# Convolution taps released one projection earlier, five to three weight units, the norm one part later

## The chip, the cores and the metric

The kernel runs on one core of a Trainium2 chip. The metric is device time in microseconds (us) of one execution, 2061.1 us as the median of three runs of the kernel before (2060.99 to 2061.4). The core has five engines that work side by side and wait for each other through semaphores: TensorE (PE) multiplies, and its weight loads (PEld) overlap its multiplications; VectorE (DVE) and ScalarE (ACT) compute element by element; GpSimd (POOL) and SyncE (SP) issue transfers here. Each engine takes its instructions in an order that is fixed before the run.

## What is computed

A trunk of two layers on 256 tokens of 2048 features. In a layer three token mixers (A sparse attention, B a convolution module, C stick-breaking attention) read the same normalised input; each is gated and projected, the three are merged by sigmoid gates, projected once more and added to the input. The branch that matters here is B:

```python
def conformer_conv(u, conv_w, conv_b, ln_w, ln_b):
    a, gt = jnp.split(u, 2, axis=-1)
    y = a * jax.nn.sigmoid(gt)
    y = lax.conv_general_dilated(y, conv_w, window_strides=(1,), padding=[(CONV_WIDTH - 1, 0)],
                                 feature_group_count=CONV_CH) + conv_b      # depthwise, width 31
    y = layer_norm(y, ln_w, ln_b)
    return jax.nn.silu(y)

def hybrid_layer(x, ...):
    proj = rms_norm(x, norm_w) @ w_in
    (qa, ka, va, za, qi, ki, wi, ub, zb, qc, kc, vc, zc, gates) = jnp.split(proj, split_points(), axis=-1)
...
    y_a = (dsa_attention(qa, ka, va, qi, ki, wi, top_k) * jax.nn.silu(za)) @ w_a_out
    y_b = (conformer_conv(ub, ...) * jax.nn.silu(zb)) @ w_b_out
    y_c = (stick_breaking_attention(qc, kc, vc) * jax.nn.silu(zc)) @ w_c_out
    g = jax.nn.sigmoid(gates).reshape(b, s, N_BRANCH, D_MODEL)
    merged = g[:, :, 0] * y_a + g[:, :, 1] * y_b + g[:, :, 2] * y_c
    return x + merged @ w_out
```

The convolution has 1024 channels, which are 8 blocks of 128 partitions, and 31 taps: 248 products of a block with a tap's column of weights, in each layer. A final norm closes the trunk.

## The kernel before

**Weight units.** All weights are streamed once, in units of mostly 512 KB. `load_unit` (L193) issues a unit's transfer on SyncE's queue into one of four `raw` buffers. `high` (L216) rounds it on ACT into `wh`, and `low` (L220) subtracts on DVE what is left into `wl` (L222); three buffers of each. The products (L232, through `mult`) of a unit use `wh` twice, for the high and the low part of the activations, and `wl` once. `chunk_T` (L235), `chunk_N` (L332) and `chunk_first` (L302) run a projection over its units; a projection of 512 columns over the 2048 features has eight units of twelve matmuls. `unit` and its parts carry high priority.

**Work beside the units.** The order of each engine is made before the run by the framework's scheduler: what is ready is placed, high priority first, otherwise what was written earlier first. `tc.issue_after(ins)` ties the instructions of its block, as far as they are on `ins`'s engine, behind `ins`. Three lists bring work in between the units:
- `pending` (L142): what follows a `turned` projection. Its result is transposed in blocks on DVE, written to memory and read back on POOL's queue, and then used some ten units later.
- `stages` (L134): generators that `background` (L156) moves on by one part after a unit, each part asking for so many units before the next; their matmuls are tied behind the unit's last matmul. `finish` runs all that are left.
- `waiting` (L132): the convolution's taps. `taps` (L663) makes, for four of the eight channel blocks, the 124 calls in the order pair of blocks, tap, block of the pair, and cuts them into entries of two and one. `tap` (L420) is one DVE instruction of 128 x 256 elements: L424 for a block's first tap, L426 for the thirty that follow and add to the same accumulator `cv`. `drain` (L174) is called by `low` and issues one entry for each unit, tied behind that unit's subtraction, unless `hold` is set. `flush` (L185) issues all entries that are left, untied.

**The order of a layer.** First the two halves of the convolution's input (UG and UA, 512 columns each); `use_u` (L674) copies each half into `yT` (L675) and calls `taps`. Then `hold` is set (L700), and the indexer's queries QI (32 units of 256 columns, matmuls of 384 and 192 columns), its keys, the values VA and the keys KA of branch A follow. `index_first` and `index` (L735, L763) are stages that score the keys and pick the top 64 by eight rounds of a maximum and a replacement on DVE (`choose`, L727). Beside them run QA (the sparse branch's queries) and QC (the stick branch's), 16 units each. Then `hold` is cleared (L799), and KC, the gate ZA and VC follow (16 units each), with `attend` (L801) and `stick` (L865) as stages. Last the merge (L953): for each branch, in the order A, C, B, four parts `j` of 512 columns; a part has eight units of the gate and four of the branch's output projection. The gate ZC (16 units) stands ahead of branch A's last part, and ZB ahead of branch C's last part (`b == 2 and j == 3`). `flush` and the start of `conv_norm` (L913) stand ahead of branch C's second part (`b == 2 and j == 1`, L963).

**`conv_norm`.** A stage of three parts: sums over the channel blocks (L918, L919); three units later a matmul that makes the mean (L922), the subtraction (L925), squares and their sums (L928, L929); six units later the matmul for the variance (L932) and the rest. Its result in `cv` is what ZB's gate is multiplied with.

Of the kernel before, what the change touches and what calls it, by code (L numbers as in the profile page):

```python
# [48 lines left out]
def trunk(ctx: ExitStack, tc: tile.TileContext, x, w_in, xt, w_a, w_b, w_c, w_out,  # L49
# [38 lines left out]
    def nm(s):  # L88
        uid[0] += 1
        return f"{s}_{uid[0]}"  # L90

    def slot(dt=F32):
        return sp.tile([P, KC, S], dt, tag="s8", bufs=12, name=nm("s8"))
# [7 lines left out]
    def parts(n, own=()):  # L101
        own = list(own)
        return own + [slot(F32R).rearrange("p (k w) t -> p k w t", w=2) for _ in range(n // 4 - len(own))]
# [22 lines left out]
    def ev():  # L126
        return tp.tile([P, 512], F32, tag="ev", bufs=3, name=nm("ev"))

    def small(w=16, bufs=8):
        return tp.tile([P, w], F32, tag=f"sm{w}", bufs=bufs, name=nm("sm"))  # L130

    waiting = []  # L132
# [19 lines left out]
    def settle():  # L152
        while pending:
            step_on(pending[0])
# [10 lines left out]
    def start(gen):  # L165
        stages.append([gen, 0])

    def finish():
        while stages:
            advance(stages[0])  # L170

    hold = [False]
# [10 lines left out]
            it[0] -= 1  # L183

    def flush():  # L185
        while waiting:
            for f in waiting.pop(0)[1]:
                f()

    newest = [None]  # L190
    newest_parts = [None, None]
# [62 lines left out]
    def turned(srcs, use, later=LATER, tmp=None):  # L254

        n = len(srcs)
        if tmp is None:
            tmp = tp.tile([P, n * 512], F32, tag="zt", bufs=1, name=nm("zt"))  # L260
        tmp = tmp.rearrange("p (t b k i) -> p t b k i", b=4, k=4, i=32)
        z = dp.tile([n, 4, 32, 4, P], F32, tag="z", bufs=4, name=nm("z"))
        with tc.high_priority():
            for t, src in enumerate(srcs):
                nc.vector.transpose(tmp[:, t].rearrange("p b k i -> p k b i"),  # L265
                                    src.rearrange("p (k b c) -> p k b c", b=4, c=32))
            for a in range(4):
                nc.gpsimd.dma_start(z[:, :, :, a, :].rearrange("t b c e -> c (t b) e"),  # L268
                                    tmp[a * 32:(a + 1) * 32].rearrange("c t b k i -> c (t b) (k i)"))

        def rest():
            y = tp.tile([P, n * 4, 4, 32], F32, tag="zy", bufs=1, name=nm("zy"))
            nc.gpsimd.dma_start(y.rearrange("p (t a) k i -> p t (a k i)", t=n),  # L273
                                z.rearrange("t b c a e -> (b c) t (a e)"))
            yield later - 2
            yield from use(y)

        pending.append([count[0] + 2, rest()])
# [7 lines left out]
    def chunk_F(w, c0, act, nk, use, later=LATER):  # L286
        turned(chunk_N(w, [(c0, 512)], act, nk), use, later)
# [44 lines left out]
    def chunk_N(w, segs, act, nk, ku=2, accs=None, ks=None):  # L332
        n = sum(c for _, c in segs)
        if accs is None:
            accs = token_accs()
        for k0 in range(*(ks or (0, nk)), ku):
            background(token_products(accs, n, unit(w, k0, ku, segs), act, k0, ku, nk, range(NT)))
        return accs
# [70 lines left out]
    def gate(c0, o, b, w, hx):  # L409
        def use(k, y):  # L410
            sg = sigmoid_of(y)
            yield 1
            nc.vector.tensor_mul(y, y, sg)
            nc.vector.tensor_mul(y, y, blocks(o[:, k:k + 4, :]).rearrange("p k u i -> p u k i"))
            split(blocks(hi(b, k, 4)), blocks(lo(b, k, 4)), by_feature(y))

        for k in range(0, KC, 4):
            chunk_F(w, c0 + k * P, hx, KD, partial(use, k), LATER + 1 if k else LATER - 1)
# [55 lines left out]
    for layer in range(DEPTH):  # L474
# [188 lines left out]
        def taps(j, yT=yT, cv=cv, pr=pr):  # L663
            ops = []
            for c in range(j * 4, j * 4 + 4, 2):
                for q in range(TAPS):
                    for d in range(2):
                        ops.append(partial(tap, yT, cv, pr, c + d, q))
            while ops:
                n = 1 + (len(waiting) % 2 == 0)  # L670
                waiting.append([4, ops[:n]])
                ops = ops[n:]

        def use_u(j, y, yT=yT):  # L674
            nc.scalar.copy(blocks(yT[:, j * 4:j * 4 + 4, PAD:]), by_feature(y))  # L675
            taps(j)
            yield 0
# [109 lines left out]
        qaT = slot()  # L787
        for h in range(0, NH, 4):
            chunk_F(w, O_QA + h * P, hx, KD, partial(rope_F, qaT[:, h:h + 4, :]), LATER - 1)
        qcT = slot()  # L790

        def use_q(h, y, qcT=qcT):
# [3 lines left out]
        for h in range(0, NH, 4):  # L796
            chunk_F(w, O_QC + h * P, hx, KD, partial(use_q, h))
        finish()
        hold[0] = False  # L799

        def attend(t, c, qaT=qaT, kaT=kaT, va=va, bias=bias):  # L801
            n = (t + 1) * P
# [110 lines left out]
        def conv_norm(cv=cv, pr=pr):  # L913
            work = t4()
            red = [work[:, i * S:(i + 1) * S] for i in range(4)]
            sums = red[2:]
            for i in range(2):
                nc.vector.tensor_reduce(red[i], cv[:, i * 4:i * 4 + 4, :].rearrange("p c t -> p t c"), op=ALU.add, axis=AX.X)  # L918
            nc.vector.tensor_add(red[0], red[0], red[1])  # L919
            yield 3  # L920
            ps = mm_tile()
            nc.tensor.matmul(ps[:, :S], mean_w, red[0], start=True, stop=True)  # L922
            for i in range(2):
                cs = cv[:, i * 4:i * 4 + 4, :]
                nc.vector.tensor_sub(cs, cs, heads(ps[:, :S], 4))  # L925
                sq = t4()
                nc.scalar.activation(sq.rearrange("p (c t) -> p c t", c=4), cs, AF.Square)
                nc.vector.tensor_reduce(sums[i], sq.rearrange("p (c t) -> p t c", c=4), op=ALU.add, axis=AX.X)  # L928
            nc.vector.tensor_add(sums[0], sums[0], sums[1])  # L929
            yield 6  # L930
            vs = mm_tile()
            nc.tensor.matmul(vs[:, :S], mean_w, sums[0], start=True, stop=True)  # L932
            r = rsqrt_mean(vs[:, :S], 1, t4())
            for i in range(2):
                cs = cv[:, i * 4:i * 4 + 4, :]
                nc.vector.tensor_mul(cs, cs, heads(r, 4))
                sg = t4()
                for c in range(4):
                    cc = i * 4 + c
                    lw, lb = pr[:, P_LW + cc:P_LW + cc + 1], pr[:, P_LB + cc:P_LB + cc + 1]  # L940
                    nc.scalar.activation(sg[:, c * S:(c + 1) * S], cs[:, c, :], AF.Sigmoid, bias=lb, scale=lw)
                    nc.vector.tensor_scalar(cs[:, c, :], cs[:, c, :], lw, lb, op0=ALU.mult, op1=ALU.add)
                nc.vector.tensor_mul(cs, cs, sg.rearrange("p (c t) -> p c t", c=4))
# [9 lines left out]
        for b in (0, 2, 1):  # L953
            if b == 1:
                mx = parts(KD)
            gx = ga if b == 0 else gc if b == 2 else gb
            for j in range(4):

                if b == 0 and j == 3:
                    finish()  # L960
                    gc = parts(KC)
                    gate(O_ZC, qcT, gc, w, hx)
                if b == 2 and j == 1:  # L963
                    flush()
                    start(conv_norm())
                if b == 2 and j == 3:
                    finish()
                    gb = parts(KC)
                    gate(O_ZB, cv, gb, w, hx)
                g = chunk_N(w, [(O_G + b * D + j * 512, 512)], hx, KD)  # L970
                sg = [ev() for _ in range(NT)]
                with tc.high_priority():
                    for t in range(NT):
                        nc.scalar.activation(sg[t], g[t], AF.Sigmoid)  # L974
                if j == 0:
                    settle()
                y = chunk_N((w_a, w_b, w_c)[b][layer], [(j * 512, 512)], gx, KC)
                with tc.high_priority():
                    for t in range(NT):
                        dst = mg[j // 2][:, j % 2, t, :]  # L980
                        if b == 0:
                            nc.vector.tensor_mul(dst, y[t], sg[t])
                        else:
                            nc.vector.tensor_mul(sg[t], y[t], sg[t])  # L984
                            nc.vector.tensor_add(dst, dst, sg[t])  # L985
                if b == 1:
                    turned([mg[j // 2][:, j % 2, t, :] for t in range(NT)], partial(use_m, j), LATER - 2)
# [58 lines left out]
        c0, n = 1536, 256  # L1046
# [8 lines left out]
        c0, n = D - S, S  # L1055
# [5 lines left out]
        for t in range(NT):  # L1061
# [4 lines left out]
            m, r, b = (small(1) for _ in range(3))  # L1066
# [66 lines left out]
```

## Time and profile before

| | us |
|---|---|
| median of three runs | 2061.1 |
| the profiled execution | 2062.56 |
| its span, from the first to the last instruction | 2060.8 |
| PE busy in it | 2035.9 |
| DVE busy in it | 1504.4 |
| taps (L426, 480 in two layers) | 218.8, 478 ns each |
| subtractions (L222, the 729 of the main group) | 876.6, 1207 ns each |

The page lists busy times, the chain of waits that ended last, and the groups of instructions. A line of the timeline is start, duration, engine, line, operation, tiles written from tiles read, shape and count; in brackets stands how long the engine was idle before it, and what ended the wait. Several like instructions in a row are merged into one line with a count (`x6`). A stretch of the view by windows is its length and then, for each engine, busy time and count. Matmuls are pipelined, so that the duration of one is longer than the distance from its start to the next one's.

### The profile page before, as it was taken

What the parts mean: (1) busy time and instruction counts of PE and PEld (TensorE: products, weight loads), DVE (VectorE), ACT (ScalarE), POOL (GpSimd) and SP (SyncE); (2) the same over time, 40 slices, a digit from 0 to 9 for tenths busy, and PEclk for the clock granted to TensorE, in tenths of its full rate; (3) what the DMA queues carried; (4) which work ended last, traced back from release to release, by engine and by line L of the source; (5) the groups of instructions that cost most, each with busy time, mean ns of one, the idle gap of its engine ahead of it and who ended that gap; (6) DMA issues with size and microseconds to landing.
All of it is one profiled execution on the core that took longest, in us unless ns stands there. A gap on an engine that the chain in (4) does not pass through costs nothing.

```text
span 2060.8 us, 26151 instructions
## 1 busy us (share of the span) xinstructions
PE 2035.9 (99%) x9680; PEld 1721.7 (84%) x9680; DVE 1504.4 (73%) x2020; ACT 1042.1 (51%) x1223; POOL 119.2 (6%) x199
## 2 busy tenths in 40 slices
PE   9999999999999999999999899999999999999998
PEld 8889888888888788888888898888888887888887
DVE  8687878787778956555775879777886799566555
ACT  7455545466444544444554554554664445444443
POOL 0100011100010000010100000111000100000100
PEclk9999999999999999999999999999999999999999
DMA  7767586765576577776967675867655765676764
GB/s 264 226 201 225 179 245 194 234 191 168 175 234 194 174 217 236 213 234 215 307 200 232 184 212 184 247 185 233 195 164 181 233 189 182 214 250 212 245 223 152
DMA packets 246528, 435.03 MB, mean 211 GB/s; under 512 B 19712, under 2 KB 69888, under 8 KB 246272
## 3 DMA queue, kind: packets, MB, share of 16 engines
q1 hardware_dynamic: 231632, 389.32, 60.5%
q0 software_dynamic: 13104, 40.91, 6.5%
q10 hardware_dynamic: 1664, 3.15, 0.4%
q8 instruction: 75, 1.23, 0.2%
q14 instruction: 53, 0.43, 0.1%
HBM read 408.67 MB, written 24.64 MB: 210 GB/s over the span
## 4 chain that ended last, share of the span: by engine, by line
PE 94%; DVE 4%; issue 1%; ACT 0%; DVEq 0%; ACTq 0%
PE acc L232 90%; DVE wl L222 2%; DVE s L426 2%; PE mm L772 1%; PE mm L806 1%; PE mm L831 0%; PE mm L904 0%; PE mm L868 0%; PE mm L823 0%; PE mm L604 0%; DVE t L928 0%; PE mm L890 0%; PE mm L743 0%; PE mm L871 0%; PE mm L906 0%
## 5 line engine op out<-in xcount | busy, mean ns | idle before, releaser
L232 PE MATMUL acc<-wh,s 128*128 128x512 f32 (+2 forms) x5248 | 1283.6, 387 | 0.0
L222 DVE TENSOR_TENSOR wl<-raw,wh 128x1024 fp32r<-128x1024 f32 (+2 forms) x729 | 876.6, 1207 | 426.9 <-ACT wh L218 420.5
L218 ACT CAST wh<-raw 128x1024 fp32r<-128x1024 f32 (+2 forms) x728 | 758.2, 1043 | 845.1 <-PE acc L232 653.9
L232 PEld LDWEIGHTS acc<-wh,s 128*128 128x128 f32 x5248 | 971.0, 188 | 195.1 <-ACT wh L218 0.4
L232 PE MATMUL acc<-wl,s 128*128 128x512 f32 (+2 forms) x2624 | 692.2, 386 | 0.0
L232 PEld LDWEIGHTS acc<-wl,s 128*128 128x128 f32 x2624 | 487.8, 188 | 99.2
L426 DVE SCALAR_TENSOR_TENSOR s<-yT,cst,s 128x256 f32<-128x256 f32 x480 | 218.8, 478 | 3.0
L268 POOL DMA_DIRECT2D z<-zt x152 | 88.7, 590 | 1603.3 <-DVE zt L265 1453.4
L232 PE MATMUL acc<-s,wh 128*128 128x384 f32 (+1 forms) x608 | 129.4, 355 | 0.0
L232 PEld LDWEIGHTS acc<-s,wh 128*128 128x128 f32 x608 | 107.7, 194 | 3.2
L232 PEld LDWEIGHTS acc<-s,wl 128*128 128x128 f32 x608 | 80.2, 195 | 15.3 <-DVE wl L222 14.3
L232 PE MATMUL acc<-s,wl 128*128 128x192 f32 (+1 forms) x608 | 82.4, 279 | 10.4 <-DVE wl L222 10.3
L265 DVE STREAM_TRANSPOSE zt<-acc 128x512 f32<-128x512 f32 x48 | 34.1, 711 | 17.4 <-PE acc L232 17.4
L273 POOL DMA_DIRECT2D zy<-z x39 | 28.0, 719 | 253.3 <-DMA z<-zt 100.4
L367 DVE TENSOR_TENSOR s<-zy,s 128x1024 fp32r<-128x1024 f32 x20 | 24.4, 1220 | 21.6 <-ACT s L366 21.6
L366 ACT CAST s<-zy 128x1024 fp32r<-128x1024 f32 x20 | 21.0, 1051 | 29.1 <-DMA zy<-z 23.0
L984 DVE TENSOR_TENSOR ev<-acc,ev 128x512 f32<-128x512 f32 x32 | 21.9, 685 | 13.2 <-PE acc L232 13.2
L974 ACT ACTIVATE ev<-acc 128x512 f32<-128x512 f32 x48 | 26.5, 592 | 0.1
L391 DVE TENSOR_TENSOR ev<-ev,cst 128x384 f32<-128x384 f32 (+2 forms) x20 | 11.1, 557 | 17.4 <-ACT ev L389 17.2
L388 ACT COPY ev<-ev 64x384 f32<-64x384 f32 (+2 forms) x20 | 10.2, 511 | 25.9 <-DVE ev L293 25.7
L985 DVE TENSOR_TENSOR s<-s,ev 128x512 f32<-128x512 f32 x32 | 21.8, 683 | 0.0
L1016 DVE TENSOR_TENSOR t<-acc,t 128x512 f32<-128x512 f32 (+1 forms) x18 | 10.6, 627 | 13.8 <-PE acc L232 13.8
(206 smaller groups left out, 828.8 us busy)
## 6 DMA issues: line engine op xcount, KB each, us to landing
raw<-in_w_in_dram SPq DMA_DIRECT2D x555, 512.0 KB, 3.9
raw<-in_w_out_dram SPq DMA_DIRECT2D x64, 512.0 KB, 4.7
zy<-z POOLq DMA_DIRECT2D x39, 512.0 KB, 5.3
z<-zt POOLq DMA_DIRECT2D x152, 128.0 KB, 4.1
raw<-in_w_a_dram SPq DMA_DIRECT2D x32, 512.0 KB, 3.6
raw<-in_w_c_dram SPq DMA_DIRECT2D x32, 512.0 KB, 4.0
raw<-in_w_b_dram SPq DMA_DIRECT2D x32, 512.0 KB, 4.9
raw<-in_w_in_dram SPq DMA_DIRECT2D x16, 256.0 KB, 3.1
```

Source lines behind the costliest of these rows:

```text
L218: newest_parts[0] = nc.scalar.copy(u[1], u[0])
L222: newest_parts[1] = sub = nc.vector.tensor_sub(u[2], u[0], u[1].bitcast(F32))
L232: newest[0] = nc.tensor.matmul(o, lhsT, rhs, start=start, stop=stop, skip_group_check=True)
L265: nc.vector.transpose(tmp[:, t].rearrange("p b k i -> p k b i"), src.rearrange("p (k b c) -> p k b c", b=4, c=32))
L268: nc.gpsimd.dma_start(z[:, :, :, a, :].rearrange("t b c e -> c (t b) e"), tmp[a * 32:(a + 1) * 32].rearrange("c t b k i -> c (t b) (k i)"))
L273: nc.gpsimd.dma_start(y.rearrange("p (t a) k i -> p t (a k i)", t=n), z.rearrange("t b c a e -> (b c) t (a e)"))
L366: nc.scalar.copy(h, src)
L367: nc.vector.tensor_sub(l, src, h.bitcast(F32))
L426: nc.vector.scalar_tensor_tensor(o, yT[:, c, q:q + S], wq, o, op0=ALU.mult, op1=ALU.add)
L974: nc.scalar.activation(sg[t], g[t], AF.Sigmoid)
L984: nc.vector.tensor_mul(sg[t], y[t], sg[t])
L985: nc.vector.tensor_add(dst, dst, sg[t])
```

## The change

Four places, all about the taps. `hold` is cleared after QA instead of after QC, so that entries are issued from QC's first unit on. An entry holds one tap where the length of the list divides by three, and two otherwise, which is five taps in three units instead of three in two. `flush` and the start of `conv_norm` move from branch C's second part to its third. And what `flush` issues is tied behind the newest subtraction.

```diff
     def flush():
-        while waiting:
-            for f in waiting.pop(0)[1]:
-                f()
+        with tc.issue_after(newest_parts[1].ins):
+            while waiting:
+                for f in waiting.pop(0)[1]:
+                    f()
...
             while ops:
-                n = 1 + (len(waiting) % 2 == 0)
+                n = 1 + (len(waiting) % 3 > 0)
                 waiting.append([4, ops[:n]])
                 ops = ops[n:]
...
             chunk_F(w, O_QA + h * P, hx, KD, partial(rope_F, qaT[:, h:h + 4, :]), LATER - 1)
+        hold[0] = False
         qcT = slot()
...
         for h in range(0, NH, 4):
             chunk_F(w, O_QC + h * P, hx, KD, partial(use_q, h))
         finish()
-        hold[0] = False
...
-                if b == 2 and j == 1:
+                if b == 2 and j == 2:
                     flush()
                     start(conv_norm())
```

## The prediction

> **What bounds the kernel now.** I read the page's busy times and the chain of waits first.
>
> ```profile
> span 2060.8 us, 26151 instructions
> PE 2035.9 (99%) x9680; PEld 1721.7 (84%) x9680; DVE 1504.4 (73%) x2020; ACT 1042.1 (51%) x1223; POOL 119.2 (6%) x199
> PE acc L232 90%; DVE wl L222 2%; DVE s L426 2%; PE mm L772 1%; PE mm L806 1%; PE mm L831 0%; PE mm L904 0%; PE mm L868 0%; PE mm L823 0%; PE mm L604 0%; DVE t L928 0%; PE mm L890 0%; PE mm L743 0%; PE mm L871 0%; PE mm L906 0%
> ```
>
> TensorE (PE) is the bound: 2035.9 of 2060.8 us busy, 24.9 us idle. A change of VectorE's (DVE) order can only act where PE waits for DVE. The chain says there are such places, and that the low-part subtractions (L222) and the convolution taps (L426) stand in them with 2% each. So the next view is the busy time by stretch: length, then PE, weight loads, DVE, ACT, POOL, granted clock, DMA share, GB/s.
>
> ```profile
> 112.00:146.00 34.00, 29.87 (x183) 28.08 (x182) 31.48 (x57) 16.69 (x23) 0.00 (x0) 0.90 0.54 163
> 146.00:252.00 106.00, 105.98 (x640) 96.68 (x639) 84.33 (x152) 57.66 (x79) 3.04 (x5) 1.00 0.68 205
> 252.00:296.00 44.00, 44.00 (x196) 36.44 (x195) 32.63 (x39) 21.08 (x20) 6.09 (x10) 1.00 0.81 250
> 296.00:420.00 124.00, 124.00 (x567) 102.73 (x566) 94.96 (x133) 62.74 (x88) 14.52 (x24) 1.00 0.69 210
> 420.00:560.00 140.00, 140.00 (x642) 116.68 (x641) 111.34 (x160) 85.51 (x92) 0.72 (x1) 1.00 0.57 177
> 656.00:688.00 32.00, 32.00 (x142) 26.48 (x142) 30.55 (x47) 13.22 (x14) 0.00 (x0) 1.00 0.61 193
> 688.00:704.00 16.00, 13.45 (x58) 10.53 (x57) 15.46 (x18) 8.87 (x9) 0.00 (x0) 1.00 0.48 143
> 1134.00:1170.00 36.00, 29.74 (x181) 27.95 (x181) 32.80 (x59) 17.02 (x25) 0.00 (x0) 0.91 0.54 163
> 1712.00:1728.00 16.00, 13.45 (x58) 10.54 (x58) 15.21 (x17) 8.84 (x9) 0.00 (x0) 1.00 0.47 142
> ```
>
> PE is short in two places of each layer, and full between them: among the indexer's queries (112 to 146, and 1134 to 1170 in layer 1: 4.13 and 6.26 us idle, DVE nearly full, clock 0.90), and at the convolution's norm (688 to 704 and 1712 to 1728: 2.55 us idle each). These four hold 15.5 of the 24.9 us.
>
> **Which taps stand there.** The same view for L426 alone (DVE busy and count), then lines of DVE's timeline:
>
> ```profile
> 112.00:146.00 34.00, 14.49 (x30) 0.90 0.54 163
> 656.00:688.00 32.00, 14.48 (x30) 1.00 0.61 193
> 113.86 0.41 DVE L424 TENSOR_SCALAR s<-yT,cst 128x256 f32<-128x256 f32 x1 [0.67 <-ACT yT L675]
> 122.53 1.22 DVE L222 TENSOR_TENSOR wl<-raw,wh 128x1024 fp32r<-128x1024 f32 x1
> 123.66 3.08 DVE L426 SCALAR_TENSOR_TENSOR s<-yT,cst,s 128x256 f32<-128x256 f32 x6
> 657.80 0.41 DVE L424 TENSOR_SCALAR s<-yT,cst 128x256 f32<-128x256 f32 x1
> ```
>
> One first tap (L424) and thirty followers are one channel block's whole chain of 31. It starts at 113.86, as soon as the second half of yT is copied, although `hold` is set then. Counting entries says which it is. Each half has 124 taps, in the old code 83 entries of two and one in turn. One entry goes before `hold`; 124 weight units follow its release until `flush` (KC, ZA and VC 16 each, branch A's four parts 48 with ZC's 16 between, branch C's first part 12). They issue 185 taps more, up to the first of block 6. What `flush` finds is block 7 whole (31) and 30 of block 6. `drain` ties a tap behind its unit's subtraction; `flush` ties nothing. Block 7 therefore depends on yT alone, and the scheduler, which orders each engine ahead of the run, put it into the queries. Block 6 hangs on a tied tap and stays at 657 (its thirty are the second row).
>
> **Term 1, the queries' stall, removed.** The matmul timeline, with a regular unit, a stall, and the ends of the disturbed stretch in both layers:
>
> ```profile
> 112.45 1.59 PE L232 MATMUL acc<-s,wh 128*128 128x384 f32 x8
> 121.63 1.59 PE L232 MATMUL acc<-s,wh 128*128 128x384 f32 x8
> 127.93 1.14 PE L232 MATMUL acc<-s,wl 128*128 128x192 f32 x8 [1.57 <-DVE wl L222]
> 145.96 1.59 PE L232 MATMUL acc<-s,wh 128*128 128x384 f32 x8
> 1143.43 1.59 PE L232 MATMUL acc<-s,wh 128*128 128x384 f32 x8
> 1169.87 1.59 PE L232 MATMUL acc<-s,wh 128*128 128x384 f32 x8
> ```
>
> From 112.45 to 121.63 lie four units: 2.295 us each. With six taps between two subtractions DVE needs 3.08 + 1.22 = 4.3 us for one, so PE runs dry. From 121.63 to 145.96 lie seven units in 24.33 us instead of 16.06: 8.27 lost. From 1143.43 to 1169.87 again seven, in 26.44: 10.38 lost. In the new code no entry reaches `flush`: five taps in three units make 75 entries of each half, 150 in all; one goes before `hold`, 149 remain; release before QC gives 16 units more and the later flush 12, so 152 units. Three are spare, and the tie added to `flush` has nothing to act on. Every first tap is tied, so no chain can run ahead into the queries. The queries' other DVE work left PE full from 146 on. Term 1: −18.65, bounds −10.39 (the idle alone) and −18.65.
>
> Part of term 1 is clock, not idle; rows of PE, clock, DMA share and GB/s:
>
> ```profile
> 128.00:132.00 4.00, 3.51 (x16) 0.64 0.43 131
> 132.00:136.00 4.00, 3.93 (x15) 0.50 0.43 131
> ```
>
> The granted clock falls right behind the waits of 1.6 us and nowhere in the full stretches, so I count it with them. The Trainium skill, "TensorE: Matmul & The Clock Gate", section "HAM oscillation", names idle gaps above about 3.4 us as what lowers the clock. By that rule waits this short would not be its cause, and the dips could outlast the taps: term 1 would be the idle alone, −10.39, and the time some 8.3 us higher than by the rows.
>
> **Term 2, the norm's two waits.**
>
> ```profile
> 258.03 1.07 PE L232 MATMUL acc<-wl,s 128*128 128x512 f32 x4
> 260.75 1.07 PE L232 MATMUL acc<-wl,s 128*128 128x512 f32 x4
> 688.01 0.84 PE L232 MATMUL acc<-wl,s 128*128 128x512 f32 x3
> 690.02 0.70 PE L922 MATMUL mm<-t,cst 128*128 128x256 f32 x2 [1.16 <-DVE t L919]
> 698.97 0.39 PE L232 MATMUL acc<-wh,s 128*128 128x512 f32 x1
> 700.74 0.70 PE L932 MATMUL mm<-t,cst 128*128 128x256 f32 x2 [1.39 <-DVE t L929]
> 1713.60 0.70 PE L922 MATMUL mm<-t,cst 128*128 128x256 f32 x2 [1.16 <-DVE t L919]
> 1724.33 0.70 PE L932 MATMUL mm<-t,cst 128*128 128x256 f32 x2 [1.39 <-DVE t L929]
> 690.75 1.22 DVE L925 TENSOR_TENSOR s<-s,mm 128x1024 f32<-128x1024 f32 x1 [0.54 <-PE mm L922]
> 700.27 0.42 DVE L929 TENSOR_TENSOR t<-t 128x256 f32<-128x256 f32 x1
> ```
>
> The first two rows are two units of QC, 2.72 us apart; a unit has twelve matmuls, so they start 0.227 us apart. So L922 came 690.02 − 688.01 − 3 × 0.227 = 1.33 late and L932 700.74 − 698.97 − 0.227 = 1.54: 2.87 a layer, and layer 1 shows the same waits. Block 6's thirty taps held DVE until the sums began, so the first matmul slid towards the second. After the change the last tap leaves in part 1's ninth unit; the sums run beside its last three, L922 is placed three units after part 2's first, and L932 six further, 6 × 2.72 = 16.3 us, while DVE's work between them took 690.75 to 700.69, 9.9 us. Term 2: −5.74, bounds −5.74 and 0 (both waits return one part later). The norm's tail then runs beside branch C's third part and ends long before ZB's gating product needs it, some twenty units on; I cost that at nothing.
>
> **Term 3, the taps that come into QC.** 16 units × 5/3 = 26.7 taps of 3.08 / 6 = 0.51 us: 13.7 us of DVE a layer.
>
> ```profile
> 255.75 1.22 DVE L222 TENSOR_TENSOR wl<-raw,wh 128x1024 fp32r<-128x1024 f32 x1
> 295.82 0.48 DVE L426 SCALAR_TENSOR_TENSOR s<-yT,cst,s 128x256 f32<-128x256 f32 x1
> ```
>
> The old first tap, at 295.82, marks KC's first unit; sixteen subtractions back is QC's first, at 252.8. In 252 to 296 DVE has 44 − 32.63 = 11.4 us free, the remaining 2.3 run into KC, where 124 − 94.96 = 29.0 are free. The least lead is in QC's second unit, while the top-k choice ends: ready at 256.97, used at 260.75, 3.78 us. No gain is possible there, since PE is full. If instead all the taps stood ahead of subtractions and none in the gaps, PE would lose 13.7 − 3.78 = 9.9 a layer, 19.8 in all. The nearest row is 656 to 688: three and four taps to a unit, DVE 30.55 of 32 us, and PE still full. I take 0, with 0 to +19.8 for the range. A subtraction carries high priority, so at most a tap or two gets ahead of each. The rows between KC and the flush bear one and a half taps a unit with PE full; a sixth more is 0.09 us a unit, 11 a layer, against 29.0 free in 296 to 420 and 28.7 in 420 to 560: 0. No transfer or ACT instruction is added; the SyncE queue's loads wait for the same subtractions.
>
> **Sum.** −18.65 − 5.74 + 0 = −24.4. The profiled execution took 2062.56 (span 2060.8); the median is 2061.1, 1.5 less. A span of 2036.4, and a median of 2036.7.
>
> **Rivals.**
> - QC becomes DVE's stretch: taps and choice wear down the 3.78 us of lead. Halfway to the bound above, 9.9 in all come back: 2046.6. For it: the choice already fills DVE there. Against: the full PE of 656 to 688.
> - The norm's waits return one part later: 2036.7 + 5.7 = 2042.4. For it: each reduction is as long as before. Against: the distances above.
> - The clock dips stay: 2036.7 + 8.3 = 2045.0. Against: they stand at the stalls alone.
> - It doesn't do what it says: entries remain, or another chain is issued early, and the queries stall as before: 2061. Against: the count with three spare units.
> - Slower: DVE sets the pace from QC to branch C's second part. The 61 taps that `flush` had, 61 × 0.51 = 31.1 us a layer, move into those units; uncovered but for the lead they cost 31.1 − 3.78 = 27.3 a layer, 2036.7 + 54.6 = 2091. It decides once more than 16.0 of the 31.1 us lie bare (16.0 − 3.78 = 12.2 a layer, the gain). For it: DVE is at 30.55 of 32 before the flush. Against: 11.4 + 29.0 + 28.7 us free up to 560 alone.
>
> **Chances.** Forecast 0.58, QC 0.16, norm 0.10, clock 0.05, no effect 0.05, slower 0.06. A measurement of this kernel tells about 0.2%, 4.1 us, from no change: the first four are faster, 0.89; same 0.05; slower 0.06. The range 2034 to 2050 holds the first four: below, 2.7 us for small waits that I haven't counted; above, QC's give-back somewhat past the middle. I state 2037.
>
> **What would show it.** Right: no L426 or L424 between 100 and 200 but for the pre-`hold` one; queries at 2.295 us a unit with clock 1.00; first tap after the release near 246 (QC starts some 8 us earlier); no wait at L922 and L932; PE idle near 10 us. Wrong: matmuls of QC or KC waiting for L222 with taps between subtractions; taps in a burst before the norm; the dips still there.

## The result, and the profile after

The changed kernel takes 2037.67 us in the median of four runs (2037.47 to 2037.90), the kernel before 2061.25 (2060.99 to 2062.92): 23.6 us less, a ratio of 0.9884 with a 95% interval of 0.9867 to 0.9901. In the profiled executions the span falls from 2060.8 to 2035.8, by 25.0 us; the one of the kernel before took 2062.56, some 1.4 us above the median. Most lines behind 185 are one higher than before: the products are L233, the subtractions L223, the taps L425 and L427, the norm's two matmuls L923 and L933.

The page of the changed kernel: span, busy times, the chain of waits by line.

```profile
span 2035.8 us, 26155 instructions
PE 2026.5 (100%) x9680; PEld 1717.7 (84%) x9680; DVE 1498.0 (74%) x2020; ACT 1042.8 (51%) x1223; POOL 119.2 (6%) x199
PE acc L233 96%; PE mm L773 1%; PE mm L807 1%; PE mm L832 0%; PE mm L905 0%; PE mm L869 0%; PE mm L824 0%; PE mm L605 0%; PE mm L891 0%; PE mm L744 0%; PE mm L872 0%; PE mm L907 0%; PE mm L896 0%; PE mm L893 0%; PE mm L441 0%; PE mm L923 0%
```

VectorE's subtractions and taps are gone from the chain. PE is idle for 9.3 us now. Its busy time fell too, from 2035.9 to 2026.5, with the same 9680 matmuls: part of the old loss was matmuls at a lower clock. The same stretches as in the prediction, at their new times (length, then PE, weight loads, DVE, ACT, POOL, clock, DMA share, GB/s): the queries in both layers, QC, and the norm.

```profile
100.00:138.00 38.00, 38.00 (x268) 38.00 (x267) 27.28 (x40) 24.69 (x34) 1.61 (x3) 1.00 0.81 248
244.00:288.00 44.00, 44.00 (x196) 36.44 (x195) 42.49 (x66) 21.20 (x21) 6.09 (x10) 1.00 0.79 249
684.00:704.00 20.00, 20.00 (x90) 16.56 (x89) 13.34 (x14) 8.32 (x9) 0.00 (x0) 1.00 0.63 199
704.00:720.00 16.00, 16.00 (x73) 13.23 (x72) 12.21 (x11) 9.93 (x12) 0.00 (x0) 1.00 0.59 180
1112.00:1146.00 34.00, 34.00 (x239) 34.00 (x239) 24.98 (x36) 23.09 (x31) 0.72 (x1) 1.00 0.83 259
```

PE is full in all five, at clock 1.00. DVE is lighter among the queries and fuller in QC, 42.49 of 44 us against 32.63 before.

How much each place gave can be read from matmuls that both kernels have. Three pieces of the chain, before: the indexer's first matmul in layer 0, the last transposition at the start of layer 1, the indexer's first in layer 1.

```profile
207.92 0.89 PE mm L743 x8
1035.85 0.87 PE mm L440 x8
1231.51 0.89 PE mm L743 x8
```

The same three after:

```profile
199.50 0.89 PE mm L744 x8
1024.32 0.87 PE mm L441 x8
1209.59 0.89 PE mm L744 x8
```

Up to the indexer 8.42 us are won; up to layer 1 11.53, so 3.11 between the two, where the norm lies; from there to the next indexer 21.92 − 11.53 = 10.39; and to the end 25.0 − 21.92 = 3.1. The queries gave 18.8 us and the norms 6.2.

### The profile page after: what moved, and what is told of

Its sections match the earlier page's. It is cut to its first block, busy times and chain, and to the rows that moved or that the text cites. A ratio compares the mean times of both kernels' runs of the same rounds, so it can differ in the third digit from the quotient of the medians.

```text
span 2035.8 us, 26155 instructions
## 1 busy us (share of the span) xinstructions
PE 2026.5 (100%) x9680; PEld 1717.7 (84%) x9680; DVE 1498.0 (74%) x2020; ACT 1042.8 (51%) x1223; POOL 119.2 (6%) x199
## 4 chain that ended last, share of the span: by engine, by line
PE 100%; DVE 0%; ACT 0%; DVEq 0%; issue 0%
PE acc L233 96%; PE mm L773 1%; PE mm L807 1%; PE mm L832 0%; PE mm L905 0%; PE mm L869 0%; PE mm L824 0%; PE mm L605 0%; PE mm L891 0%; PE mm L744 0%; PE mm L872 0%; PE mm L907 0%; PE mm L896 0%; PE mm L893 0%; PE mm L441 0%; PE mm L923 0%
## 5 line engine op out<-in xcount | busy, mean ns | idle before, releaser
L233 PE MATMUL acc<-wh,s 128*128 128x512 f32 (+2 forms) x5248 | 1283.9, 387 | 0.0
L223 DVE TENSOR_TENSOR wl<-raw,wh 128x1024 fp32r<-128x1024 f32 (+2 forms) x729 | 876.9, 1208 | 402.2 <-ACT wh L219 394.9
L233 PEld LDWEIGHTS acc<-wh,s 128*128 128x128 f32 x5248 | 971.4, 188 | 194.9
L233 PE MATMUL acc<-wl,s 128*128 128x512 f32 (+2 forms) x2624 | 691.5, 385 | 0.0
L233 PEld LDWEIGHTS acc<-wl,s 128*128 128x128 f32 x2624 | 487.7, 188 | 99.2
L427 DVE SCALAR_TENSOR_TENSOR s<-yT,cst,s 128x256 f32<-128x256 f32 x480 | 212.2, 478 | 0.0
L233 PE MATMUL acc<-s,wh 128*128 128x384 f32 (+1 forms) x608 | 125.6, 347 | 0.0
L233 PEld LDWEIGHTS acc<-s,wh 128*128 128x128 f32 x608 | 104.3, 189 | 3.2
L233 PEld LDWEIGHTS acc<-s,wl 128*128 128x128 f32 x608 | 79.1, 191 | 0.9
L233 PE MATMUL acc<-s,wl 128*128 128x192 f32 (+1 forms) x608 | 79.4, 273 | 0.0
L368 DVE TENSOR_TENSOR s<-zy,s 128x1024 fp32r<-128x1024 f32 x20 | 24.4, 1222 | 20.9 <-ACT s L367 20.9
L367 ACT CAST s<-ev 128x256 fp32r<-128x256 f32 x16 | 6.5, 407 | 24.4 <-DVE ev L399 24.4
```

The costliest lines, as they stand in the source:

```text
L223: newest_parts[1] = sub = nc.vector.tensor_sub(u[2], u[0], u[1].bitcast(F32))
L233: newest[0] = nc.tensor.matmul(o, lhsT, rhs, start=start, stop=stop, skip_group_check=True)
L367: nc.scalar.copy(h, src)
L368: nc.vector.tensor_sub(l, src, h.bitcast(F32))
L427: nc.vector.scalar_tensor_tensor(o, yT[:, c, q:q + S], wq, o, op0=ALU.mult, op1=ALU.add)
```

## The experiments

Each was timed over four runs beside the kernel before, except for the two repeats at the end. The queries' loss is read as above, by the indexer's first matmul.

**The tie alone.** The kernel before, with what `flush` issues tied, and nothing else.

```diff
     def flush():
-        while waiting:
-            for f in waiting.pop(0)[1]:
-                f()
+        with tc.issue_after(newest_parts[1].ins):
+            while waiting:
+                for f in waiting.pop(0)[1]:
+                    f()
```

> The kernel before with one edit: what flush issues is tied behind the newest subtraction; release, entries and the norm's place stay old. Theory (block 7's chain stood in the queries because nothing tied it): the queries' stall goes as in the changed kernel, 8.4 and 10.4 us, with no tap between the pre-hold one and KC; flush then has all 61 taps in front of the norm, four to a unit, 4 x 0.51 + 1.14 = 3.2 us of VectorE against 2.72 us of TensorE, so about 17 x 0.46 - 5.65 = 2 us a layer of new waits beside the norm's old ones of 3.1: 2061.25 - 18.8 + 4.4 = 2047, between 2042 and 2050. Rival (the early release and the thinner entries took the stall away, the tie does nothing): 2061, with taps still among the queries.

It took 2043.03 us (ratio 0.9910, 0.9895 to 0.9924). The queries were clean; the rival falls. All 61 taps stood in front of the norm, and what was to cost 2.2 us a layer there, taps that hold up subtractions, cost nothing: PE waited for no subtraction. Two lines of DVE's timeline and the norm's two matmuls show why:

```profile
663.21 1.68 DVE L427 SCALAR_TENSOR_TENSOR s<-yT,cst,s 128x256 f32<-128x256 f32 x4
664.79 1.23 DVE L223 TENSOR_TENSOR wl<-raw,wh 128x1024 fp32r<-128x1024 f32 x1
702.64 0.70 PE L923 MATMUL mm<-t,cst 128*128 128x256 f32 x2 [0.71 <-DVE t L920]
713.41 0.70 PE L933 MATMUL mm<-t,cst 128*128 128x256 f32 x2 [1.41 <-DVE t L930]
```

Four taps of two blocks in turn took 1.58 us from the first one's start to the subtraction behind them, 0.40 each, not 0.51. With 1.14 for the subtraction that makes 2.72, just what PE needs for a unit. What stays are the norm's two waits: 2.1 us a layer, 4.2 of the 5.4 us by which this kernel is slower than the changed one.

**Only the place of the norm.** The kernel before, with `flush` and the norm one part later.

```diff
-                if b == 2 and j == 1:
+                if b == 2 and j == 2:
                     flush()
                     start(conv_norm())
```

> The kernel before with one edit: flush and the norm move to branch C's third part. Twelve units more drain 18 taps, so that the first tap of block 7 leaves tied to its unit and flush finds 43 taps of chains that have begun. Theory (only a chain whose first tap is untied can run ahead): the queries' stall goes, 18.8 us, though release, entries and the missing tie are the old ones; the norm's waits stay at about 3.1 a layer: 2042.4, between 2039 and 2047. Rival (the late release, or the untied flush as such, makes the stall): the queries stall as before, 2061, or 2055 if the norm's waits go.

It took 2042.81 us (ratio 0.9908, 0.9894 to 0.9923), and PE did not wait among the queries, with the late release, the old entries and an untied `flush`. Together with the tie alone, that leaves the untied first tap as the cause. The norm's waits moved along with it:

```profile
718.84 0.70 PE L922 MATMUL mm<-t,cst 128*128 128x256 f32 x2 [0.72 <-DVE t L919]
734.32 0.70 PE L932 MATMUL mm<-t,cst 128*128 128x256 f32 x2 [1.12 <-DVE t L929]
```

So one part later is not by itself what frees the norm.

**The changed kernel with the norm at its old place.**

```diff
-                if b == 2 and j == 2:
+                if b == 2 and j == 1:
                     flush()
                     start(conv_norm())
```

> The changed kernel with flush and the norm back at branch C's second part, nothing else: 140 of 149 entries are out by then, some 15 taps are left. Theory (the norm's two waits come of the long row of leftover taps in front of it, which the fixed order of TensorE did not foresee in full): no stall in the queries, and with a quarter of the 61 taps left the waits at the mean's and the variance's matmul shrink to between 0 and half: 2038 to 2041. Rival (the norm's own reductions make the waits wherever it follows straight on the last taps): both waits back in full, 1.3 and 1.5 us a layer or more, 2037.7 + 6.2 = 2044.

It took 2039.00 us (ratio 0.9890, 0.9873 to 0.9906). With some 15 taps left in front of the norm the first wait was 0.39 us and the second gone:

```profile
667.47 0.70 PE L923 MATMUL mm<-t,cst 128*128 128x256 f32 x2 [0.39 <-DVE t L920]
684.37 0.59 PE L933 MATMUL mm<-t,cst 128*128 128x256 f32 x2
```

**The changed kernel with the late release.** Some 22 taps are left for the norm's front.

```diff
         for h in range(0, NH, 4):
             chunk_F(w, O_QA + h * P, hx, KD, partial(rope_F, qaT[:, h:h + 4, :]), LATER - 1)
-        hold[0] = False
         qcT = slot()
...
         finish()
+        hold[0] = False
```

> The changed kernel with hold cleared after QC again, nothing else: 136 of 149 entries are out before flush, some 22 taps are left for the norm's front. Theory (a row of leftover taps of this length fits into the lead; the queries are clean because no first tap is untied): no stall in the queries, norm waits between 0 and 3 a layer: 2038 to 2043. Rival (the early release is what frees the queries): 2056. If QC costs anything in the changed kernel, this one is faster by that before the norm: TensorE's first matmul of branch A's gate arrives earlier.

It took 2039.63 us (ratio 0.9894, 0.9876 to 0.9912). The queries were clean, the mean's matmul waited 0.59 us, the variance's not. It also answers whether the early release costs anything in QC: from the indexer's first matmul (L744) to branch A's first (L807) are 294.45 − 199.76 = 94.69 us here and 294.19 − 199.50 = 94.69 in the changed kernel, so the taps in QC cost nothing. Pieces of the chain, of the late release and then of the changed kernel:

```profile
199.76 0.89 PE mm L744 x8
294.45 0.89 PE mm L807 x8
```

```profile
294.19 0.89 PE mm L807 x8
```

**Two taps in every entry, and the norm at its old place.** Nothing is left over, and the norm stands where it stood before.

```diff
-                n = 1 + (len(waiting) % 3 > 0)
+                n = 2
...
-                if b == 2 and j == 2:
+                if b == 2 and j == 1:
```

> The changed kernel with two taps in every entry and flush and the norm back at branch C's second part: 123 entries after the release, 140 units before flush, so that nothing is left over and the norm stands where it stood before. Theory (the norm's two waits came of the leftover taps in front of it, not of the part in which it stands): no wait at the mean's and the variance's matmul, 2037.7, between 2037 and 2039. Rival (the later part is what frees the norm): waits of 0.4 to 1.4 us at each matmul again, 2039 to 2044. QC gets 32 taps instead of 26.7; if that stretch were short of VectorE time, waits on subtractions would appear there.

It took 2037.61 us (ratio 0.9882, 0.9867 to 0.9897), the same as the changed kernel, and neither matmul waited:

```profile
666.77 0.59 PE L923 MATMUL mm<-t,cst 128*128 128x256 f32 x2
683.56 0.59 PE L933 MATMUL mm<-t,cst 128*128 128x256 f32 x2
```

The waits came of the leftover taps, not of the part in which the norm stands.

**Three taps in every entry.** A test of how much QC and what follows can bear.

```diff
-                n = 1 + (len(waiting) % 3 > 0)
+                n = 3
```

> The changed kernel with three taps in every entry: QC's 16 units get 48 taps (24.6 us of VectorE) instead of 26.7 (13.7 us), against 11.4 us free and 3.8 us of lead; all taps are out half way through VC. Theory (the change costs nothing in QC because its taps fit into what VectorE has free, and subtractions go first): past that room waits on subtractions appear in QC, KC and ZA, where a unit with four taps needs 3.2 us and one with six 4.2 us against 2.72: 2045 to 2075. Rival (VectorE's order never matters there, since subtractions have priority): 2038, and PE full in 244 to 411.

It took 2040.63 us (ratio 0.9899, 0.9884 to 0.9915), 3 us more than the changed kernel and well below what I expected. The stretches of QC and of KC with ZA, and one line of PE's timeline:

```profile
244.00:288.00 44.00, 44.00 (x196) 36.44 (x195) 44.00 (x73) 21.17 (x21) 6.10 (x10) 1.00 0.76 239
288.00:411.00 123.00, 122.11 (x557) 100.64 (x556) 119.51 (x204) 62.09 (x88) 14.52 (x24) 1.00 0.68 214
316.83 0.47 PE L832 MATMUL mm<-ph,vah 128*128 128x512 f32 x1 [0.78 <-DVE pl L368]
```

DVE was busy 44.00 of 44 and 119.51 of 123 us, and no matmul waited for a subtraction. The scheduler put more taps off instead: 36 of L427 stand in 244 to 288, where the 16 entries hold 48 taps. What came late was attention's own work (the low part of its weights, L368). PE waited 0.8 us for it, and L807's next matmuls start 1.4 us later than in the changed kernel (324.34 against 322.92). Subtractions stayed ahead, as the rival says, but PE was not full, as the rival had it: what the taps displaced is the rest of VectorE's work.

**Taps block by block.** In the changed kernel an entry's taps mostly belong to two blocks in turn. Here they are all of one block, so that each reads what the one before it wrote.

```diff
-            for c in range(j * 4, j * 4 + 4, 2):
+            for c in range(j * 4, j * 4 + 4):
                 for q in range(TAPS):
-                    for d in range(2):
+                    for d in range(1):
                         ops.append(partial(tap, yT, cv, pr, c + d, q))
```

> The changed kernel with the taps taken block by block instead of in pairs of blocks, so that each tap reads what the tap just before it wrote. Theory from the traces so far (six taps of one block took 3.00 us from start to start, 0.50 each, four taps of two blocks in turn 1.58, 0.40 each): two taps of one entry start 0.5 us apart here and 0.4 in the changed kernel; VectorE has 0.1 to 0.2 us a unit more to do, which lies in its free time: 2037.7, up to 2039. Rival for the price (0.50 is how a tap goes behind a subtraction or in the queries, whatever block it is of): 0.4 us apart here too. Rival for the time (VectorE is near its limit from QC to VC): 2040 to 2050 with waits on subtractions.

It took 2037.76 us (ratio 0.9882, 0.9866 to 0.9899). Two taps of an entry at the same place, first here, then in the changed kernel:

```profile
403.46 1.00 DVE L427 SCALAR_TENSOR_TENSOR s<-yT,cst,s 128x256 f32<-128x256 f32 x2
```

```profile
403.35 0.88 DVE L427 SCALAR_TENSOR_TENSOR s<-yT,cst,s 128x256 f32<-128x256 f32 x2
```

A tap lasts 0.48 us in both. The pair takes 1.00 here, so that the second starts 0.52 after the first, and 0.88 there, 0.40 after. By this pair a chain of one block costs DVE some 30% more for each tap, and here that lies beneath PE's work.

**Block 7 set free again.** The changed kernel with block 7's 31 taps issued untied when `yT` is copied.

```diff
                     for d in range(2):
-                        ops.append(partial(tap, yT, cv, pr, c + d, q))
+                        if c + d == 7:
+                            tap(yT, cv, pr, c + d, q)
+                        else:
+                            ops.append(partial(tap, yT, cv, pr, c + d, q))
```

> The changed kernel with block 7's 31 taps issued untied when yT is copied, not through the entries; the other seven blocks go through the entries. Theory (term 1 is the price of one untied chain among the queries): the stall comes back as it was, 8.4 and 10.4 us, with six taps between two subtractions and a granted clock of 0.5 to 0.65 right behind the waits: 2037.7 + 18.8 = 2056.5, between 2052 and 2060. Rival (the early release makes room, or the scheduler spreads the chain over units where VectorE is free): under 2045. Second rival, on the clock: if the dips don't follow the waits, the idle comes back alone, 2037.7 + 10.4 = 2048 with the clock at 1.00.

It took 2052.84 us (ratio 0.9958, 0.9943 to 0.9972): 15.2 us of the 18.8 came back. The old pattern is there, six taps between two subtractions, and PE waiting:

```profile
122.82 3.08 DVE L427 SCALAR_TENSOR_TENSOR s<-yT,cst,s 128x256 f32<-128x256 f32 x6
125.82 1.22 DVE L223 TENSOR_TENSOR wl<-raw,wh 128x1024 fp32r<-128x1024 f32 x1
131.23 1.14 PE L233 MATMUL acc<-s,wl 128*128 128x192 f32 x8 [1.58 <-DVE wl L223]
```

The same three matmuls as in the result, by the chain of waits:

```profile
207.08 0.89 PE mm L747 x8
1031.90 0.87 PE mm L441 x8
1224.81 0.89 PE mm L747 x8
```

The queries lost 207.08 − 199.50 = 7.6 us in layer 0, and in layer 1 192.91 − 185.27 = 7.6 as well, not 8.4 and 10.4. The clock fell in layer 0 alone, and in layer 1 four waits of 1.29 to 1.57 us passed at 1.00 (PE's busy time, clock, DMA share, GB/s):

```profile
112.00:146.00 34.00, 30.48 (x190) 0.90 0.57 173
1134.00:1170.00 36.00, 30.23 (x202) 1.00 0.55 173
```

This did not fit a clock that follows the waits, so I profiled both kernels a second time, unchanged.

> The kernel before once more, unchanged, for a second profile. First reading (the dips of the granted clock are set by the waits): the clock falls to 0.5 at the same places, once in each layer, some 8 us after the first wait in layer 0 and 14 us in layer 1, for 6 us each. Second reading (they come by the phase of something that runs free of the program): other places or other lengths, with the same waits.

> The kernel with block 7 untied once more, unchanged, for a second profile. First reading: the clock falls in layer 0 for 6 us and not at all in layer 1, as in the first profile. Second reading: layer 1 has a dip this time, or layer 0 none, with the waits on the subtractions again at 1.3 to 1.6 us.

They took 2061.05 and 2053.16 us. The queries' stretches in the second profile of the kernel before (PE's busy time, clock, DMA share, GB/s), one of its waits, and the three matmuls of the chain:

```profile
112.00:146.00 34.00, 27.04 (x183) 1.00 0.57 165
1134.00:1170.00 36.00, 30.13 (x194) 0.95 0.57 165
```

```profile
136.84 1.14 PE L232 MATMUL acc<-s,wl 128*128 128x192 f32 x8 [1.94 <-DVE wl L222]
```

```profile
208.23 0.89 PE mm L743 x8
1036.12 0.87 PE mm L440 x8
1229.99 0.89 PE mm L743 x8
```

And of the second profile with block 7 free, the stretches and the three matmuls:

```profile
112.00:146.00 34.00, 28.32 (x190) 1.00 0.59 175
1134.00:1170.00 36.00, 31.66 (x201) 0.95 0.57 169
```

```profile
207.50 0.89 PE mm L747 x8
1032.38 0.87 PE mm L441 x8
1225.18 0.89 PE mm L747 x8
```

The first reading falls: the kernel before had a dip in layer 0 in one execution and none in the next, and the kernel with block 7 free had one in layer 0 alone and then in layer 1 alone, each time with waits of the same kind. That something with a phase of its own sets the dips, as the second reading supposes, is not shown.

A dip that lies inside DVE's row costs nothing. Without it layer 0's queries of the kernel before were not shorter: from the first stalled matmul (123.80, and 124.08 in the second profile) to the indexer are 84.12 us with the dip and 84.15 without, with PE busy 29.87 and 27.04 us. With block 7 free layer 1 took 192.91 us without a dip and 1225.18 − 1032.38 = 192.80 with one. DVE set the pace there, and a slow PE only fills what would have been idle. Where the dip outlasts DVE's row it does cost: in layer 1 of the kernel before from 1035.85 to 1231.51 are 195.66 us in the first profile (clock 0.91 in its stretch) and from 1036.12 to 1229.99 193.87 in the second (0.95), against 185.27 in the changed kernel. So 1.8 of the 2.8 us that did not come back in layer 1 are a dip; the other 1.0, and 0.8 in layer 0, were not traced.

## Why the prediction was right

The predicted 2037.0 and the measured 2037.67 differ by 0.7 us. The mechanism is the predicted one; that the number fits so closely is in part luck, as the point on the sum shows. By its steps:

- **Term 1, the queries: −18.65 predicted, −18.8 measured.** The cause is shown from both sides: tying what `flush` issues, or draining block 7's first tap in time, clears the queries without anything else of the change, and setting it free alone brings most of the stall back. The seven units counted in 24.33 and 26.44 us were the right measure, since they hold idle and clock together.
- **The sum: 1.5 us taken off twice.** The terms were read from a profiled execution of 2062.56, and the sum then took 1.5 off for the way to the median, as if the changed kernel's profile would lie as far above its own median. The second profile of the kernel before, one execution of 2061.05 and so at the median, has a span 1.5 us shorter, and its layer 1 is 1.8 us shorter up to the indexer. The excess was the longer dip, and term 1 had removed it already with its 10.38. From profile to profile 25.0 us were won, on medians 23.6, and the sum said 24.4. The 1.5 counted twice, the 0.6 that terms 1 and 2 were too small, and the step from 2036.7 to the stated 2037 nearly cancel.
- **Its lower bound and the clock rival were wrongly built.** "Part of term 1 is clock, not idle": I took the idle time as one part of the loss and the slow clock as another, so that either could go without the other. In a stretch that DVE paces they stand in for each other: without the dip the idle is larger by as much. Only the part of a dip that outlasts the row costs, some 1.8 us between the two profiles of layer 1. In the changed kernel the clock is 1.00 in both queries' stretches, and nothing of the rival's 8.3 us is left. And the dip does not stand "right behind the waits" in each execution.
- **Term 2, the norm: −5.74 predicted, −6.2 measured.** The leftover taps are shown as the cause: no leftovers, no wait, at the old place as well as at the new. That the norm comes one part later matters only because twelve more units drain before it. The missing 0.2 us a layer are the slower start after a wait, which I had left out. Before, the next product started 701.09 − 700.74 = 0.35 us after the variance's first matmul; after the change 699.78 − 699.54 = 0.24 us after the mean's, with no wait. Twice 0.11 makes the difference. The product behind L932 before, and the mean's matmul with the product behind it after:

```profile
701.09 1.99 PE L232 MATMUL acc<-wh,s 128*128 128x512 f32 x7
```

```profile
699.54 0.59 PE L923 MATMUL mm<-t,cst 128*128 128x256 f32 x2
699.78 2.19 PE L233 MATMUL acc<-wh,s 128*128 128x512 f32 x8
```

- **Term 3, the taps in QC: 0 predicted, 0 measured.** Its working was too dear: taps of two blocks in turn start 0.40 us apart, so 26.7 of them in such a row are 10.7 us and not 13.7. The lead in QC of layer 0 never fell below 3.45 us. The thinnest place, in DVE's and PE's timelines of the changed kernel:

```profile
245.82 0.40 DVE L425 TENSOR_SCALAR s<-yT,cst 128x256 f32<-128x256 f32 x1
250.41 1.18 DVE L223 TENSOR_TENSOR wl<-raw,wh 128x1024 fp32r<-128x1024 f32 x1
255.04 1.07 PE L233 MATMUL acc<-wl,s 128*128 128x512 f32 x4
```

  The subtraction ends at 251.59, and its first matmul starts at 255.04. The first tap after the release stands at 245.82, where it was expected near 246. The rival's bound of 9.9 us a layer supposed that taps would stand ahead of subtractions in any number; with three taps in every entry the loss was 1.4 us a layer and stood elsewhere.
- **The count.** 149 entries for 152 units left `flush` nothing to do. Built without the new tie the changed kernel is the same program: the tie is a safeguard here. In the kernel before it clears the queries alone, as the first experiment shows, but not the norm's waits.
- **The slower rival** fell because the 61 taps found room: from QC up to 690 us DVE's busy time stayed below PE's in every stretch, 42.49 of 44 at most.

No version beat the changed kernel: two taps an entry with the norm at its old place comes out the same. Of the 9.3 us that PE still idles, none is a wait on a tap.

## What to carry to other kernels

Background work that a scheduler may place by readiness needs its first instruction tied, because a chain hangs where its head hangs; a leftover list that is issued without the tie of its siblings can turn up far ahead of where it is written. Look for work of that kind at places where the text does not put it: here a line counted in stretches showed 30 taps where the code holds them back. Size a stall by the length of the stretch between two instructions that both kernels have, not by the idle time of the engine that waits.

## What the runs showed of the hardware

Two taps on VectorE, of 128 x 256 elements each, start 0.40 us apart when the second does not read what the first wrote, and 0.50 to 0.52 when it does, although one of them lasts 0.48 in both cases.

The granted clock fell to 0.50 after two to four waits of 0.6 to 1.9 us, which left PE busy for some 60 to 70% of the time, in some executions and layers and not in others with the same waits: five waits of up to 1.94 us passed at clock 1.00 in layer 0 of the second profile of the kernel before. The Trainium skill, "TensorE: Matmul & The Clock Gate", section "HAM oscillation", names idle gaps above about 3.4 us as the condition; here the clock fell with no gap as long as 2 us, and the measurement decides. What makes it fall in one execution and not in the next was not tried.
